# Copies of the transposed activations on VectorE, and later copies, earlier loads and an earlier PSUM layout on the way into a decoder's RWKV-7 scan

## The chip, the core and the metric

One NeuronCore of a Trainium2 chip runs the whole program. The metric is device time in microseconds (us), from start to end of one execution. The core's engines are TensorE (PE in the profile; PEld is its weight load), VectorE (DVE), ScalarE (ACT), GpSimd (POOL) and SyncE (SP), which here issues nearly all DMAs. Each engine runs its own instructions in order; semaphores order the engines against each other.

## The reference

A decoder trunk of two layers in float32, for one sequence of 1024 tokens with 1024 channels. Each layer adds three blocks to the residual x, each between two RMS norms:

```python
x += post_norm(mixer(pre_norm(x)))             # layer 0: RG-LRU, layer 1: RWKV-7
x += post_norm(mem_xattn(pre_norm(x), norm(mem)))
x += post_norm(sqrelu_mlp(pre_norm(x)))        # square(relu(h @ w_up)) @ w_down
```

The RWKV-7 mixer of layer 1 mixes each token with the one before it, and projects the mixes to r, k and v. The decay, the rate a and the gate come from small low-rank maps. Then there is a state of 64×64 for each of 16 heads, and a recurrence over all tokens:

```python
xx = x_prev - x
r = (x + xx * mu[0]) @ w_rkv[0]
k = (x + xx * mu[2]) @ w_rkv[1]
v = (x + xx * mu[3]) @ w_rkv[2]
...
sa = einsum('bhij,bhj->bhi', state, a_t)
state = state * w_t + sa * b_t + v_t * k_t     # outer products
y_t = einsum('bhij,bhj->bhi', state, r_t)
```

## The kernel before, in words

**Arithmetic and buffers.** Each float32 operand of a matrix product is split into a high part (a cast, L233 on ScalarE) and a low part (the difference, L234 on VectorE); a product is three matmuls, high by high (L318), high by low (L319) and low by high (L320). The working buffers are one pool of 45 units u of 128×1024 floats and two large tiles z. PSUM is used in pairs of banks (p, 128×1024) and in single banks (q, 128×512).

**Order of the work.** The program is one straight stream of instructions; a scheduler with a model of the engines reorders each engine's queue, within the data dependences and within constraints such as `behind()`, which lets what is written in it be issued only after what the program has so far. Weights come in the order in which they are used: `self.depth` says for how many weights ahead the split may run and `self.ahead` how many more may be loaded (L249, a DMA on SyncE). `DA = (2, 1)` holds in k and r.

**The seam.** The last product of layer 0's MLP leaves its result transposed tile by tile. For each 128 tokens `tail` computes an RMS norm (L327 squares and sums on ScalarE, L329 and L331 on GpSimd take the root), scales (L673), adds the residual row block that L654 has loaded (L674), stores it (L675), takes a second norm and scales (L681). Every four such blocks go to `transpose_in`: TensorE transposes them (L359) into eight PSUM banks of 128×512, and from each bank ScalarE writes the high part (L362) and, as `raw` is given here, a whole copy into z (L364); the low part comes from GpSimd for odd k (L366, from the copy) and from VectorE for even k (L368, from PSUM). So there are first transposes (tokens 0 to 511) and second ones. They feed the low-rank maps (q, L318 to L320; L1292 copies a result out of PSUM).

**k, r and v.** `rwkv_make_mix` makes the token mixes from the raw tiles z (L1217 on ScalarE, L1220 on VectorE, then the split). `fphase` computes 128 output channels at a time, f = 0 to 7, with 48 matmuls into one pair of banks. k runs in seven turns (`TURNS`, the last with f = 6 and 7), r in six, v in seven. In k, L1349 and L1350 take a result from PSUM; then come decays (stored by L1341), and Gram matrices (L1405, L1406; stored by L1412 and L1413), from which 32×32 triangular systems are solved on GpSimd, and the last set of them on VectorE in small steps (L1433, L1435). In r, L1519 takes a result from PSUM, times the decay that L1515 has loaded, and L1520 stores it.

**The steps beside.** `aside(step)` is called after every turn, and starts those of the steps below whose number stands in the table: `SL`, `SO` and `ST` give the turns in which the four sets are loaded, solved and stored, `ML`, `ME` and `MS` those of the merges (loads L1458 to L1460, matmuls L1472 and L1479). `solve_store` is a copy on ScalarE (L1445, 64×1024) and two stores on SyncE (L1446, L1447).

```python
SL, SO, ST = (2, 5, 8, 9), (2, 5, 8, 9), (5, 8, 12, 13)
```

**The scan** goes in 16 chunks of 64 tokens. For a pair of chunks n, `load` fetches keys (L1624) and the mixed values (L1627, into z), `load_solved` the solved systems (L1638), and `load_late` the values of v and the gates (L1651, L1655), all on SyncE. In v they stand behind the stores L1596 of each phase. GpSimd scales the next chunk's keys (L1668), TensorE forms its Gram matrices (L1679), and the state is read (L1796), solved (L1802) and updated (L1809); L1816 and the copy L1818 give the chunk's output. With PSUM layout "banks" the scan has two sets of four banks, even chunks' outputs in one, odd chunks' in the other; "mixed", which follows for the output projection, keeps the first set and makes two pairs of the rest.

## Time and profile before

| | |
|---|---|
| three runs | 2873.09, 2865.99, 2872.57 us; median 2872.57 |
| the profiled execution | 2871.51 us |
| its span, first to last instruction | 2869.8 us |
| mean granted TensorE clock | 0.993 |
| TensorE busy | 2779.0 us (97%) |
| VectorE, ScalarE, GpSimd busy | 1845.2, 1431.3, 913.3 us |
| idle before the second transposes (TensorE, 1324.84) | 4.58 us |
| idle before r (1488.66), before v (1604.07) | 2.13, 3.63 us |
| idle in the scan (1777.50) | 5.54 us |

How to read it: a row of a timeline gives the start in us from the span's start, the duration, the engine, the line of the kernel, the operation, what it writes and reads, and in brackets how long the engine had been idle and what ended that. "x4" merges neighbours of the same kind. A duration may overlap the next start, since engines are pipelined. SPq is SyncE issuing a DMA; its duration is the issue, not the transfer.

### The profile page before, as it was taken

Reading aid. Unit: us, or ns where it says so; the run is one execution under the profiler, and the core shown is the slowest. Engines: PE = TensorE matmul, PEld = TensorE weight load, DVE = VectorE, ACT = ScalarE, POOL = GpSimd, SP = SyncE. Lnnn points to the kernel's source line nnn. Section 1 sums busy time; section 2 is a strip of 40 time slices with the busy share of each in tenths; the row PEclk is TensorE's granted clock in tenths of the full one; section 3 lists DMA queues with packets and bytes.
Section 4 is the critical chain, followed back from the end, with each engine's and each line's share of the span. In section 5 each row is a group of like instructions: output and inputs, shape, how many; then the busy total and the mean of one; then the engine's idle time right before and its main releaser. Section 6 shows DMA issues by size and latency. Waiting matters only on the chain.

```text
span 2869.8 us, 42738 instructions
## 1 busy us (share of the span) xinstructions
PE 2779.0 (97%) x16955; PEld 2320.8 (81%) x16955; DVE 1845.2 (64%) x2004; ACT 1431.3 (50%) x2203; POOL 913.3 (32%) x962
## 2 busy tenths in 40 slices
PE   7999999999999999998999898999999999999998
PEld 6888788888888888887777687888888888888886
DVE  5577556557455577886575834785665655467778
ACT  5456344546544543438562544663463644555333
POOL 2000114023666500013188223863303276640001
PEclk9999999999999999999999999999999999999999
DMA  8212352323445654433557798963132255464453
GB/s 263 74 45 81 100 168 74 103 81 103 157 152 161 213 188 165 154 111 103 166 158 199 194 254 244 236 164 103 63 106 91 88 171 161 139 240 167 147 176 118
DMA packets 383592, 421.92 MB, mean 147 GB/s; under 512 B 91184, under 2 KB 294176, under 8 KB 383392
## 3 DMA queue, kind: packets, MB, share of 16 engines
q1 hardware_dynamic: 371360, 379.19, 43.7%
q0 software_dynamic: 11568, 39.41, 3.8%
q8 instruction: 133, 2.18, 0.3%
q14 instruction: 67, 0.55, 0.1%
q10 hardware_dynamic: 464, 0.59, 0.1%
HBM read 283.79 MB, written 134.74 MB: 146 GB/s over the span
## 4 chain that ended last, share of the span: by engine, by line
PE 81%; DVE 5%; POOL 3%; ACT 3%; DMA 3%; issue 3%; SPq 2%; ACTq 0%; DVEq 0%; POOLq 0%
PE q L318 17%; PE q L320 17%; PE q L319 17%; PE p L318 8%; PE p L320 8%; PE p L319 8%; PE q L1679 1%; DMA u<-d 1%; DVE u L234 1%; POOL u L1435 1%; ACT u L233 1%; DMA u<-in_b_w_rkv 1%; POOL w L1433 1%; PE q L1796 1%; ACT u L327 1%
## 5 line engine op out<-in xcount | busy, mean ns | idle before, releaser
L234 DVE TENSOR_TENSOR u<-u,u 128x1024 fp32r<-128x1024 f32 (+1 forms) x602 | 809.2, 1375 | 370.9 <-ACT u L233 342.2
L233 ACT CAST u<-u 128x1024 fp32r<-128x1024 f32 (+1 forms) x602 | 591.8, 1020 | 436.6 <-DVE u L1060 224.5
L318 PE MATMUL q<-u,u 128*128 128x512 f32 (+1 forms) x1952 | 744.2, 383 | 5.3 <-ACT u L233 2.4
L319 PE MATMUL q<-u,u 128*128 128x512 f32 (+1 forms) x1952 | 745.8, 382 | 0.5 <-POOL u L366 0.5
L320 PE MATMUL q<-u,u 128*128 128x512 f32 (+1 forms) x1952 | 740.4, 382 | 0.8 <-DVE u L234 0.8
L318 PE MATMUL p<-u,u 128*128 128x512 f32 (+1 forms) x1472 | 554.9, 379 | 18.9 <-DVE u L1519 5.6
L319 PE MATMUL p<-u,u 128*128 128x512 f32 (+1 forms) x1472 | 552.9, 376 | 3.6 <-DVE u L234 3.6
L320 PE MATMUL p<-u,u 128*128 128x512 f32 (+1 forms) x1472 | 552.2, 375 | 3.4 <-DVE u L234 3.4
L329 POOL TENSOR_SCALAR s<-s 128x1 f32<-128x1 f32 x98 | 43.1, 440 | 1268.6 <-ACT u L327 1266.9
L318 PEld LDWEIGHTS q<-u,u 128*128 128x128 f32 x1952 | 367.0, 188 | 77.3 <-ACT u L233 3.5
L320 PEld LDWEIGHTS q<-u,u 128*128 128x128 f32 x1952 | 366.9, 188 | 72.1 <-DVE u L234 1.0
L319 PEld LDWEIGHTS q<-u,u 128*128 128x128 f32 x1952 | 367.0, 188 | 71.6 <-POOL u L366 1.0
L318 PEld LDWEIGHTS p<-u,u 128*128 128x128 f32 x1472 | 280.8, 191 | 72.8 <-ACT u L233 10.6
L320 PEld LDWEIGHTS p<-u,u 128*128 128x128 f32 x1472 | 280.9, 191 | 55.0 <-DVE u L234 5.6
L319 PEld LDWEIGHTS p<-u,u 128*128 128x128 f32 x1472 | 280.9, 191 | 54.5 <-DVE u L234 7.6
L441 POOL TENSOR_TENSOR u<-u,u 128x512 f32<-128x512 f32 x120 | 186.0, 1555 | 8.9 <-PE q L319 5.1
L1118 DVE TENSOR_TENSOR z<-z,q 128x512 f32<-128x512 f32 x192 | 130.6, 683 | 80.9 <-PE q L320 80.9
L318 PE MATMUL q<-z,u 128*128 128x512 f32 x320 | 124.9, 390 | 1.6 <-ACT u L233 1.6
L319 PE MATMUL q<-z,u 128*128 128x512 f32 x320 | 124.5, 389 | 0.0
L320 PE MATMUL q<-z,u 128*128 128x512 f32 x320 | 124.2, 389 | 0.0
L442 POOL TENSOR_TENSOR u<-u 128x512 f32<-128x512 f32 x40 | 76.0, 1899 | 145.3 <-DVE u L234 73.1
L1015 POOL TENSOR_TENSOR u<-u,u 128x512 f32<-128x512 f32 x32 | 46.0, 1438 | 176.3 <-ACT u L1004 166.4
(250 smaller groups left out, 3332.7 us busy)
## 6 DMA issues: line engine op xcount, KB each, us to landing
u<-d SPq DMA_DIRECT2D x194, 512.0 KB, 4.7
d<-u SPq DMA_DIRECT2D x109, 512.0 KB, 3.3
d<-u POOLq DMA_DIRECT2D x68, 512.0 KB, 3.5
d<-u SPq DMA_DIRECT2D x132, 256.0 KB, 3.7
u<-in_m_w_up SPq DMA_DIRECT2D x64, 512.0 KB, 5.4
u<-in_m_w_down SPq DMA_DIRECT2D x64, 512.0 KB, 7.9
u<-in_c_w_kv SPq DMA_DIRECT2D x32, 512.0 KB, 6.4
u<-in_b_w_rkv SPq DMA_DIRECT2D x24, 512.0 KB, 6.7
```

Of the source, the lines that this page charges most:

```text
L233: self.nc.scalar.copy(hv, src)
L234: (eng or self.nc.vector).tensor_tensor(lv, src, hv, ALU.subtract)
L318: mm(o, ah, bh, start=first, stop=False, **kw)
L319: mm(o, ah, bl, start=False, stop=False, **kw)
L320: mm(o, al, bh, start=False, stop=last, **kw)
L327: nc.scalar.activation(junk, src, AF.Square, accum_out=ss)
L329: nc.gpsimd.tensor_scalar(v, ss, 1.0 / n, eps, ALU.mult, ALU.add)
L441: sub = lambda o, x, y: nc.gpsimd.tensor_tensor(o, x, y, ALU.subtract)
L442: nc.gpsimd.tensor_tensor(s[:, a], f1[:, a], f1[:, b], ALU.add)
L1015: tt(s1, r21, r22, ALU.add)
L1118: nc.vector.tensor_add(to_, to_, o)
L1433: eng.tensor_tensor(tv, xv_[:, 0:n, s:s + 1].broadcast_to([128, n, m]), Lv[:, s:s + 1, s + 1:].broadcast_to([128, n, m]), ALU.mult)
```

## The change

Six edits, at five places of the program:

1. In the seam, the whole copies move from ScalarE to VectorE: all eight of the first transposes, every second one (even k) of the second.
2. `solve_store` of the first two sets is called a turn later.
3. In k's turn 5 (f = 5) one more weight may be loaded ahead.
4. In r's turn 4 (f = 5) likewise.
5. The scan's `load(1)` is called after v's turn with f = 6 and `load_solved(1)` behind v's last turn; in chunk 0 only `load_late(1)` is left.
6. The PSUM layout "mixed" is made ahead of chunk 15 and not behind the scan.

```diff
@@ transpose_in
             nc.scalar.activation(h, o, AF.Copy, scale=gc)
             if raw is not None:
-                nc.scalar.activation(raw(k), o, AF.Copy, scale=gc)
+                if k in copies:
+                    nc.vector.tensor_scalar(raw(k), o, gc, None, ALU.mult)
+                else:
+                    nc.scalar.activation(raw(k), o, AF.Copy, scale=gc)
@@ tail, turn
-            xt.append(self.transpose_in(xs, nextg, None if raw is None else (lambda k: raw[hf][:, k, :])))
+            xt.append(self.transpose_in(xs, nextg, None if raw is None else (lambda k: raw[hf][:, k, :]),
+                                        copies=range(0, KT, 1 + hf)))
@@ tables
-SL, SO, ST = (2, 5, 8, 9), (2, 5, 8, 9), (5, 8, 12, 13)
+SL, SO, ST = (2, 5, 8, 9), (2, 5, 8, 9), (6, 9, 12, 13)
@@ k
+        self.depth, self.ahead = DA if i != 5 else (DA[0], DA[1] + 1)
         self.fphase(I["b_w_rkv"][0, 1], fs, xk, prep)
@@ r
+        self.depth, self.ahead = DA if i != 4 else (DA[0], DA[1] + 1)
         self.fphase(I["b_w_rkv"][0, 0], fs, xr, evac_r, spread=i == 0)
@@ v and scan
         if fs[-1] == 6:
             load_solved(0)
+            load(1)
+    with self.behind():
+        load_solved(1)
...
     for c in range(16):
+        if c == 15:
+            self.psum_layout("mixed")
         if c % 2 == 0:
             with (ExitStack() if c else self.behind()):
-                load(c // 2 + 1)
-                load_solved(c // 2 + 1)
+                if c:
+                    load(c // 2 + 1)
+                    load_solved(c // 2 + 1)
                 load_late(c // 2 + 1)
...
     post_norm(15)
     self.depth, self.ahead = 2, 3
-    self.psum_layout("mixed")
```

In the changed program the same code stands a few lines further down: L368 is L371, L673 is L677, L1217 is L1221, L1349 is L1353, L1445 is L1449, L1515 is L1520 and L1520 is L1525. VectorE's copy is L365.

VectorE's queue at the first transposes; q are the transposed PSUM banks, z_7699 the raw tile, and colt holds the gain. Before:

```order
L1118 TENSOR_TENSOR z_7700<-z_7700,q_9462 128x512
L368 SCALAR_TENSOR_TENSOR u_9959<-q_9963,colt,u_9955 128x512
L368 SCALAR_TENSOR_TENSOR u_9960<-q_9979,colt,u_9956 128x512
L368 SCALAR_TENSOR_TENSOR u_9961<-q_9995,colt,u_9957 128x512
L368 SCALAR_TENSOR_TENSOR u_9962<-q_10011,colt,u_9958 128x512
L673 SCALAR_TENSOR_TENSOR u_10027<-z_7700,s_10032,u_5461 128x1024
```

And now, at the same place of VectorE's queue:

```order
L365 TENSOR_SCALAR z_7699<-q_9963,colt 128x512
L371 SCALAR_TENSOR_TENSOR u_9959<-q_9963,colt,u_9955 128x512
L365 TENSOR_SCALAR z_7699<-q_9964,colt 128x512
L365 TENSOR_SCALAR z_7699<-q_9979,colt 128x512
L371 SCALAR_TENSOR_TENSOR u_9960<-q_9979,colt,u_9956 128x512
L365 TENSOR_SCALAR z_7699<-q_9980,colt 128x512
L365 TENSOR_SCALAR z_7699<-q_9995,colt 128x512
L371 SCALAR_TENSOR_TENSOR u_9961<-q_9995,colt,u_9957 128x512
L365 TENSOR_SCALAR z_7699<-q_9996,colt 128x512
L365 TENSOR_SCALAR z_7699<-q_10011,colt 128x512
L371 SCALAR_TENSOR_TENSOR u_9962<-q_10011,colt,u_9958 128x512
L365 TENSOR_SCALAR z_7699<-q_10012,colt 128x512
```

Eight copies have come between and behind the four low parts, and the eight L364 are gone from ScalarE's queue there; L677 (L673 before) follows.

ScalarE's queue towards the end of k, before: L1445 is the first set's copy, the casts after it are weights, p are the results of f = 6 and 7.

```order
L1358 ACTIVATE u_11508<-u_11503 128x1024
L1445 COPY u_10994<-u_10995 64x1024
L233 CAST u_11641<-u_11440 128x1024
L233 CAST u_11647<-u_11639 128x1024
L1217 ACTIVATE u_11701<-z_7699,omu 128x512 x2
L1217 ACTIVATE u_11706<-z_7699,omu 128x512 x2
L233 CAST u_11711<-u_11701 128x1024
L233 CAST u_11715<-u_11706 128x1024
L1349 ACTIVATE u_11775<-p_11651,nkk 128x1024
L1349 ACTIVATE u_11778<-p_11652,nkk 128x1024
```

And now on ScalarE, where the dots leave out the next mixes:

```order
L1362 ACTIVATE u_11510<-u_11505 128x1024
L233 CAST u_11638<-u_11440 128x1024
L233 CAST u_11644<-u_11446 128x1024
L1221 ACTIVATE u_11698<-z_7699,omu 128x512 x2
L1221 ACTIVATE u_11703<-z_7699,omu 128x512 x2
L233 CAST u_11708<-u_11698 128x1024
L233 CAST u_11712<-u_11703 128x1024
L1353 ACTIVATE u_11772<-p_11648,nkk 128x1024
L1353 ACTIVATE u_11775<-p_11649,nkk 128x1024
...
L1362 ACTIVATE u_11892<-u_11772 128x1024
L1449 COPY u_10994<-u_10995 64x1024
L233 CAST u_11911<-u_11642 128x1024
```

The copy has moved behind the casts, the mixes and the two results, some 25 instructions further back.

SyncE's queue in r around the weights (in_b_w_rkv); the DMAs with d as source are loads of what the kernel has stored, L1458 to L1460 the merge's. Before:

```order
L249 DMA u_12515<-in_b_w_rkv 128x8x128
L1520 DMA d_10150<-u_12513 128x1024
L1459 DMA u_12660<-d_10155 32x16x32
L1460 DMA u_12660<-d_10152 32x512
L1458 DMA u_12658<-d_10154 32x16x32 x4
L1459 DMA u_12660<-d_10155 32x16x32
L1460 DMA u_12660<-d_10152 32x512
L1486 DMA d_10146<-u_12346 128x1024
L1515 DMA u_12670<-d_10149 128x1024
L1515 DMA u_12672<-d_10149 128x1024
L249 DMA u_12674<-in_b_w_rkv 128x8x128
L249 DMA u_12680<-in_b_w_rkv 128x8x128
```

And now on SyncE:

```order
L249 DMA u_12515<-in_b_w_rkv 128x8x128
L249 DMA u_12521<-in_b_w_rkv 128x8x128
L1525 DMA d_10150<-u_12513 128x1024
L1463 DMA u_12662<-d_10155 32x16x32
L1464 DMA u_12662<-d_10152 32x512
```

The first of the two L249 behind the merge loads now stands ahead of them, right behind the L249 before.

More of the change, by code (lines that the diff above doesn't have):

```diff
@@ L347, in half, with transpose_in @@
         return [(at(h, k), at(l, k)) for k in range(KT)]
-    def transpose_in(self, xs, g, raw=None, dst=None):
+    def transpose_in(self, xs, g, raw=None, dst=None, copies=()):
         nc = self.nc
```

## The prediction

> **What bounds the kernel now.** I read the page first, then TensorE's timeline over the stretches that the change touches, then the other engines' timelines back from each wait of TensorE.
>
> ```profile
> span 2869.8 us, 42738 instructions
> PE 2779.0 (97%) x16955; PEld 2320.8 (81%) x16955; DVE 1845.2 (64%) x2004; ACT 1431.3 (50%) x2203; POOL 913.3 (32%) x962
> ```
>
> TensorE is busy 2779.0 of 2869.8 us, and the change takes no matmul away. So all it can win is idle time of TensorE, 90.8 us in the whole span, and whatever a wait costs behind itself. TensorE's timeline where the change acts:
>
> ```profile
> 1324.84 4.62 PE L359 MATMUL q<-ident,u 128*128 128x128 f32 x24 [4.58 <-ACT u L1292]
> 1330.19 1.09 PE L359 MATMUL q<-ident,u 128*128 128x128 f32 x8 [0.74 <-DVE u L368]
> 1332.50 0.50 PE L318 MATMUL q<-u,u 128*128 128x512 f32 x1 [1.22 <-DVE u L368]
> ...
> 1488.66 0.51 PE L318 MATMUL p<-u,u 128*128 128x512 f32 x1 [2.13 <-DVE u L1350]
> 1488.97 0.63 PE L319 MATMUL p<-u,u 128*128 128x512 f32 x1
> 1489.39 0.63 PE L320 MATMUL p<-u,u 128*128 128x512 f32 x1
> ...
> 1492.61 0.39 PE L319 MATMUL p<-u,u 128*128 128x512 f32 x1
> 1492.84 0.39 PE L320 MATMUL p<-u,u 128*128 128x512 f32 x1
> ...
> 1519.10 0.47 PE L318 MATMUL p<-u,u 128*128 128x512 f32 x1 [1.18 <-DVE u L1519]
> ...
> 1599.23 1.20 PE L1472 MATMUL q<-u 32*32 32x32 f32 x64
> 1604.07 0.47 PE L318 MATMUL p<-u,u 128*128 128x512 f32 x1 [3.63 <-DVE u L1519]
> ...
> 1777.50 2.08 PE L1679 MATMUL q<-z,u 64*128 64x128 f32 x16 [5.54 <-DMA u<-d]
> ...
> 1920.64 0.50 PE L318 MATMUL p<-u,u 128*128 128x512 f32 x1 [0.92 <-ACT u L1818]
> ```
>
> The number in brackets is TensorE's idle time and what ended it: 4.58 us in the seam, 2.13 between k and r, 3.63 between r and v, 5.54 in the scan, 0.92 at its end. There is a second price. Behind the 2.13 us gap matmuls start 0.42 us apart (1488.97, 1489.39), later 0.23 apart (1492.61, 1492.84): some eight or nine run at half rate, 9 × 0.2 = 1.8 us more. The matmuls behind the 1.18 us at 1519.10 start at that pace too, so removing most of a gap without getting below about 1 us does not win this back.
>
> [...]
>
> **Part 1, copies to VectorE.** The seam's first transposes end a chain that leads to the second ones:
>
> ```profile
> 1295.25 0.69 ACT L362 ACTIVATE u<-q,colt 128x512 fp32r<-128x512 f32 x1 [1.58 <-PE q L359]
> ...
> 1304.39 1.18 ACT L327 ACTIVATE u<-z 128x1024 f32<-128x1024 f32 x1
> 1304.69 1.30 POOL L366 TENSOR_TENSOR u<-z,u 128x512 fp32r<-128x512 f32 x1 [1.03 <-ACT z L364]
> 1306.94 1.29 DVE L673 SCALAR_TENSOR_TENSOR u<-z,s,u 128x1024 f32<-128x1024 f32 x1 [2.69 <-POOL s L331]
> 1310.14 2.35 DVE L674 TENSOR_TENSOR u<-u,u 128x1024 f32<-128x1024 f32 x2
> 1318.00 1.23 DVE L674 TENSOR_TENSOR u<-u,u 128x1024 f32<-128x1024 f32 x1 [0.21 <-DMA u<-d]
> 1323.87 0.75 DVE L681 TENSOR_SCALAR u<-u,s 128x1024 f32<-128x1024 f32 x1 [0.72 <-POOL s L331]
> L390 DVE TENSOR_SCALAR u<-q,colt x16: 741/746/751, 383.9 to 2253.3; 128x512 f32<-128x512 f32 x16
> L368 DVE SCALAR_TENSOR_TENSOR u<-q,colt,u 128x512 fp32r<-128x512 f32 x8 | 6.0, 751 | 10.3 <-ACT z L364 10.3
> ```
>
> ScalarE runs 16 instructions from 1295.25, 0.57 us apart (16 × 0.57 = 9.1, to 1304.39), and only then the squares L327 that the next RMS norms wait for. Eight fewer bring L327 forward by 8 × 0.57 = 4.6 us. VectorE takes eight copies, of the form of L390 (0.746 us), between its four L368 (0.751 us). At full length 12 × 0.75 = 9.0 us, to 1304.3; with the 0.1 us by which neighbours overlap (two L674 take 2.35, one 1.23) 12 × 0.65 = 7.8, to 1303.1. Both are before 1306.94, where L673 starts now. I take 1303.1: the first L673 moves by 3.8 us; the second, at its end, by 4.6 us, and so does the first pair of L674 at 1310.14. Its stores, the loads of the residual rows behind them on SyncE, the L674 at 1318.00 that waits for such a load, and the last L681 follow. GpSimd has four L366 of 1.30 us either way; in the new order the small rsqrt steps stand between them, so they don't wait for the last.
>
> In the second transposes ScalarE has three instructions a pair instead of four; over three pairs 3 × 0.57 = 1.7 us of the 0.74 + 1.22 = 1.96 us of waits for L368. Sum for the seam 4.6 + 1.7 = **6.3 us**. Bounds: 3 (12 full-length DVE operations give 1304.3, 2.6 us, and a little of the rest) and 8 (4.58 + 0.74 + 1.22 is 6.5, and 1.5 of half rate behind them).
>
> Do the copies slow GpSimd, or it them? The nearest rows:
>
> ```profile
> 1500.82 1.64 DVE L234 TENSOR_TENSOR u<-u,u 128x1024 fp32r<-128x1024 f32 x1
> ...
> 1597.78 1.22 DVE L234 TENSOR_TENSOR u<-u,u 128x1024 fp32r<-128x1024 f32 x1 [6.68 <-ACT u L233]
> ```
>
> L234 takes 1.64 us while the solves run on GpSimd and 1.22 alone. The same third on 12 operations would be 12 × 0.65 × 0.34 = 2.7 us; that too is inside the bound of 3. I take nothing, since the copy reads one operand from PSUM, like L368, which kept 0.75 beside L366. [...]
>
> **Part 2, the solves' copies a turn later; part 3, a weight more ahead in k.** ScalarE and VectorE between k and r:
>
> ```profile
> 1476.62 2.06 ACT L1445 COPY u<-u 64x1024 f32<-64x1024 f32 x1 [11.26 <-POOL u L1435]
> ...
> 1484.45 2.08 PE L1405 MATMUL q<-u,u 64*64 64x64 f32 x64
> 1485.71 2.11 ACT L1349 ACTIVATE u<-p,nkk 128x1024 f32<-128x1024 f32 x2
> 1487.36 2.29 DVE L1350 TENSOR_TENSOR u<-u,p 128x1024 f32<-128x1024 f32 x2
> 1489.56 3.29 DVE L1220 SCALAR_TENSOR_TENSOR u<-z,colt,u 128x511 f32<-128x511 f32 x4
> ...
> 1517.75 2.34 DVE L1519 TENSOR_TENSOR u<-u,p 128x1024 f32<-128x1024 f32 x2
> ```
>
> ScalarE stands 11.26 us at L1445 for GpSimd's solve, with the casts, the mixes L1217 and the evacuations L1349 queued behind it; TensorE waits for L1350 behind those. In the new order L1445 is behind all of them. The second L1349 then starts when its matmuls are done, at 1484.45 (TensorE's L1405, 2.08 us, begins there and ends at 1486.53). Now it starts at 1485.71 + 2.11 / 2 = 1486.76, and the first L1350 at 1487.36; one turn of L1349 alone, the first long done, leaves L1350 off TensorE's path. VectorE's mixes L1220 start when the second L1349 is over, 1484.45 + 1.05 = 1485.5, and the first of their inputs is there, about 1486, not 1489.56: **3.6 us**, by VectorE's own chain, which I take to be full up to the L1519 of 1517.75. The gap of 2.13 us and its 1.8 us of half rate give 3.9, so VectorE's chain, not TensorE, sets this. Bounds 2 (the gap goes, the half rate stays) and 5.5 (1.18 at 1519.10 shrinks below 1 us, with half its 1.8). The stall at 1519.10 stays: L1519 remains in VectorE's order behind the same work. L1445's own 2.06 us and its two stores go to a time where the solve's readers are turns away: nothing; 2 us if ScalarE is then needed. The extra weight in k, loaded ahead of SyncE's L1341 and L1394, sets the next cast's input early; no cast waited for one there (the idle 11.26 us is L1445's), so alone it is worth nothing, and its risk is the slower rival.
>
> **Part 4, a weight more ahead in r.**
>
> ```profile
> 1573.39 0.43 SPq L249 DMA_DIRECT2D u<-in_b_w_rkv  x1
> ...
> 1588.80 1.41 SPq L249 DMA_DIRECT2D u<-in_b_w_rkv  x2
> 1596.70 1.05 ACT L233 CAST u<-u 128x1024 fp32r<-128x1024 f32 x1 [12.27 <-DMA u<-in_b_w_rkv]
> ...
> 1602.70 1.22 DVE L1519 TENSOR_TENSOR u<-u,p 128x1024 f32<-128x1024 f32 x1
> 1607.84 1.21 DVE L1519 TENSOR_TENSOR u<-u,p 128x1024 f32<-128x1024 f32 x1
> ```
>
> The cast of v's weight holds ScalarE 12.27 us, then VectorE 6.68 us (the row of 1597.78), and the L1519 that frees PSUM for v is behind them. One of the two L249 of 1588.80 now stands right behind that of 1573.39, 15 us sooner, though it may wait for its buffer. At the 7.9 us from issue to cast (1588.80 to 1596.70) the cast could come at 1582; ScalarE and VectorE then do the mixes, while TensorE is still in r. L1519 of a phase can run when its matmuls are done, the last at 1599.23: I put the first at 1598.5 to 1599.5 instead of 1602.70 and the second, behind it and a few mixes, at about 1604. TensorE could go on at 1600.43, when L1472 ends (1599.23 + 1.20): 3.63 us plus 1.8 us of half rate is 5.4; VectorE's mixes are late next, so I take **4 us**, bounds 0 and 7.
>
> **Part 5, scan loads.**
>
> ```profile
> 1761.07 5.77 SPq L1627 DMA_DIRECT2D z<-d  x4
> ...
> 1770.65 6.49 SPq L1624 DMA_DIRECT2D u<-d  x4
> 1777.62 1.04 POOL L1668 TENSOR_TENSOR u<-u,pc 128x512 f32<-128x512 f32 x1 [7.38 <-DMA u<-d]
> ```
>
> Chunk 2's rows L1624 take 6.49 us to issue, and start 9.6 us after L1627; TensorE and GpSimd wait for them. Issued during v's sixth phase they have landed, and only L1655 and L1651 are left there. On SyncE they go past the stores L1596 of two phases, whose readers come only in the scan: nothing, or 2 us if a buffer isn't free yet. The whole 5.54 us goes. A 5.54 us gap costs at least the half rate that stands behind 2.13 us, 1.8. Sum **7.3 us**, bounds 5 (the 7.3 less such 2 us) and 8.
>
> **Part 6, the PSUM layout moved** ahead of the last chunk takes the 0.92 us at 1920.64 away; the last chunk has fewer banks, and may wait 1 us for one, under a VectorE that is late anyway: **0.9 us**, bounds −1 and 1.
>
> Sum: 6.3 + 3.6 + 4 + 7.3 + 0.9 = 22.1 us. The profiled execution took 2871.5 us and the three runs 2866.0 to 2873.1, median 2872.6; 2871.5 − 22 is 2849.5, and from the median 2850.4: I say **2850**. Bounds of the terms together: all low 9 us (2863), all high 29.5 us (2842).
>
> **The rivals.** *Half comes off:* the next late thing stands right behind. VectorE's mixes, in an order that still has L1519 behind them, take back what k, r and v gained; the scan and the seam's lower bound remain: 7.3 + 3 + 0.9 = 11 us, **2860**. For it: the stall at 1519.10, where L1519 is late behind VectorE's own work. Against: at 1604.07 L1519 was late behind a load (12.27 us at the cast), and that goes.
>
> *No change:* TensorE's early starts are given back where data comes at fixed times, as at the scan's DMA: **2870**. Against: the scan's own wait goes too.
>
> *Slower:* the extra L249 finds no free buffer and holds SyncE's queue until a phase of matmuls has freed one. In r everything between the L249 of 1573.39 and those of 1588.80 stands behind it: L1520, the merge loads and L1515. L1472 at 1599.23 needs the merge loads; issued by 1588.80 and with 7.9 us to land they have 1599.23 − 1588.80 − 7.9 = 2.5 us to spare, and from there each microsecond of the hold is one of TensorE. Held until r's last matmuls are done, 15 us later than the turn before, it costs some 15 us; in k the same extra weight stands ahead of the Gram stores which the solves read, and a hold of one phase, 48 matmuls × 0.23, costs 11. Seam, scan and end still give 6.3 + 7.3 + 0.9 = 14.5: 2871.5 + 26 − 14.5, **2883**. For it: 45 buffers are shared by everything. Against: SyncE issued both L249 of 1588.80 in 1.41 us, without a wait.
>
> **How the numbers follow.** Under 0.3% (8.6 us) this kernel's runs can't tell a change. Forecast 0.63, half 0.20, no change 0.11, slower 0.06. Faster by over 0.3% (under 2864) is 0.63 + 0.20 = 0.83; same 0.11, slower 0.06. The range runs from 2840 (all terms high, and 2 us for runs that differ by 7) to 2863 (all terms low, which holds the half rival), and leaves out the last two, 0.17.
>
> **What would show it.** Right: TensorE's 4.58, 2.13, 3.63 and 5.54 us gaps are below 1 us or gone, the seam's first L327 starts right behind eight L362, L1445 stands behind L1349, no 12 us wait at a cast before v, and 1.18 at 1519 stays. Wrong: a new wait of TensorE over 3 us, a SyncE hole behind the extra L249, or copies over 0.9 us.

## The result, and the profile after

The changed kernel takes 2861.62 us (median of 12 runs, 2858.27 to 2868.18); the kernel before took 2872.17 beside it (12 runs, 2865.99 to 2876.83). The ratio is 0.9966, 95% interval [0.9958, 0.9975]: 0.34% faster, 10.5 us where 22 were forecast. The profiled execution took 2861.18 us, its span is 2859.5 us against 2869.8.

To see where the 10.5 us come from, I follow single matmuls: the same one in both traces bounds a stage, and what the stage has become shorter is the gain there. These are the busy times by stage, of the kernel before, in its stages: the seam, k, r, r's last merge matmuls, r's end to the first part of v, v's end, the scan. The columns are the stage, its length, the busy time of TensorE, its weight load, VectorE, ScalarE and GpSimd with their instructions, the granted TensorE clock, DMA share and rate.

```profile
1282.79:1333.76 50.97, 42.85 (x210) 35.05 (x208) 32.16 (x38) 33.71 (x59) 23.84 (x31) 0.97 0.57 185
1333.76:1478.80 145.04, 144.17 (x964) 113.81 (x963) 95.87 (x99) 94.70 (x128) 55.57 (x72) 1.00 0.50 141
1478.80:1571.55 92.75, 87.43 (x604) 71.34 (x602) 63.08 (x67) 37.51 (x49) 75.80 (x104) 0.96 0.62 175
1571.55:1593.70 22.15, 20.44 (x265) 16.55 (x264) 18.63 (x30) 4.51 (x7) 14.96 (x25) 1.00 0.73 192
1593.70:1657.73 64.03, 54.66 (x414) 42.16 (x412) 49.81 (x76) 41.17 (x57) 7.94 (x12) 0.97 0.77 207
1657.73:1741.60 83.87, 81.89 (x915) 68.23 (x914) 27.60 (x30) 35.36 (x51) 21.19 (x33) 0.98 0.92 247
1741.60:1920.64 179.04, 166.46 (x3276) 146.68 (x3274) 122.00 (x227) 101.16 (x395) 113.38 (x132) 0.98 0.95 227
```

And of the changed kernel, between the same matmuls:

```profile
1282.54:1329.94 47.40, 43.43 (x209) 34.66 (x208) 40.75 (x51) 27.68 (x49) 24.10 (x31) 0.96 0.61 199
1329.94:1481.04 151.10, 147.70 (x964) 116.08 (x963) 103.49 (x108) 98.56 (x132) 57.81 (x74) 0.98 0.50 139
1481.04:1570.61 89.57, 85.87 (x604) 70.12 (x602) 54.58 (x56) 33.51 (x42) 78.08 (x107) 0.98 0.60 168
1570.61:1596.11 25.50, 22.77 (x266) 18.66 (x264) 24.57 (x41) 12.20 (x18) 10.56 (x19) 0.87 0.81 223
1596.11:1649.94 53.83, 52.04 (x413) 41.41 (x412) 43.09 (x68) 33.80 (x48) 7.92 (x12) 1.00 0.87 248
1649.94:1735.76 85.82, 83.37 (x915) 69.53 (x914) 27.59 (x30) 35.30 (x51) 21.12 (x33) 0.96 0.89 243
1735.76:1909.13 173.37, 166.58 (x3276) 147.00 (x3274) 120.56 (x227) 100.07 (x393) 111.88 (x131) 0.98 0.96 226
```

The lengths differ by −3.6, **+6.1**, −3.2, **+3.3**, **−10.2**, +2.0 and −5.7 us; what follows, up to the matmul at 2239.77 us (2229.05 now), adds 0.8, and the sum is −10.5. Length less PE busy is idle time. Where PE busy grows with the same number of matmuls I count the growth as half rate: the clock column falls with it (k 1.00 to 0.98, the merge 1.00 to 0.87), and in k the granted clock is 0.50 from 1429.10 to 1435.93. So k lost 2.5 us to waiting (0.87 to 3.40 idle) and 3.5 to half rate (144.17 to 147.70). So two losses, of 6.1 us in k and 3.3 at r's merge, stand there that no term of the sum held.

TensorE's waits in the changed kernel, in the timeline:

```profile
1322.63 1.14 PE L359 MATMUL q<-ident,u 128*128 128x128 f32 x8 [0.65 <-ACT u L1296]
...
1429.16 1.64 PE L1332 MATMUL q<-u,u 64*128 64x512 f32 x5 [3.40 <-DVE u L1410]
...
1502.92 0.50 PE L319 MATMUL p<-u,u 128*128 128x512 f32 x1 [1.86 <-DVE u L234]
...
1519.76 0.47 PE L318 MATMUL p<-u,u 128*128 128x512 f32 x1 [1.25 <-DVE u L1524]
...
1576.90 1.89 PE L1476 MATMUL q<-u 32*32 32x32 f32 x62 [2.73 <-DMA u<-d]
...
1601.64 1.20 PE L1476 MATMUL q<-u 32*32 32x32 f32 x64
1602.77 0.50 PE L318 MATMUL p<-u,u 128*128 128x512 f32 x1
...
1711.42 0.22 PE L1483 MATMUL q<-u,u 32*32 32x32 f32 x2 [2.11 <-issue]
...
1774.25 0.45 PE L1796 MATMUL q<-u,u 128*64 128x64 f32 x2 [2.25 <-DMA u<-d]
```

The four waits that were to go (4.58, 2.13, 3.63, 5.54 us) are 0.65 us or gone; v's first matmul at 1602.77 waits for nothing. In their place stand 3.40 us in k at the matmuls behind the Gram matrices, 2.73 at r's merge for a load, 2.11 at v's end that the profile puts down to "issue" (nothing that it shows), and 2.25 in the scan for a load.

At the wait in k, TensorE needs a bank that VectorE frees: L1406 (L1410 in the changed kernel) takes the Gram matrices out of PSUM, times small decays db that a load brings. First the kernel before, then the changed one:

```profile
1432.83 1.29 DVE L1406 TENSOR_TENSOR u<-q,db 128x512 f32<-128x512 f32 x2 [6.81 <-DMA db<-d]
1433.58 0.97 PE L1328 MATMUL q<-u,u 64*128 64x512 f32 x5 [0.87 <-DVE u L1406]
...
1428.41 1.29 DVE L1410 TENSOR_TENSOR u<-q,db 128x512 f32<-128x512 f32 x2 [6.84 <-DMA db<-d]
```

In both kernels VectorE starts 12.0 us behind the start of the Gram matrices (1420.87 and 1416.43). So the load has not become later; what differs is how much work TensorE has meanwhile.

### The profile page after: what moved, and what is told of

It is laid out like the page before. It is cut to its first block, busy times and chain, and to the rows that moved or that the text cites. A ratio compares the mean times of both kernels' runs of the same rounds, so it can differ in the third digit from the quotient of the medians.

```text
span 2859.5 us, 42726 instructions
## 1 busy us (share of the span) xinstructions
PE 2782.0 (97%) x16955; PEld 2322.7 (81%) x16955; DVE 1850.8 (65%) x2016; ACT 1424.5 (50%) x2191; POOL 912.0 (32%) x962
## 4 chain that ended last, share of the span: by engine, by line
PE 87%; DVE 4%; ACT 3%; issue 2%; POOL 2%; DMA 1%; SPq 1%; DVEq 0%; POOLq 0%; ACTq 0%
PE q L318 17%; PE q L319 17%; PE q L320 17%; PE p L318 9%; PE p L320 9%; PE p L319 9%; PE q L1685 1%; DVE u L234 1%; ACT u L233 1%; PE q L1796 1%; PE q L1808 1%; PE q L1332 1%; POOL s L331 1%; ACT u L952 1%; PE q L1709 1%
## 5 line engine op out<-in xcount | busy, mean ns | idle before, releaser
L234 DVE TENSOR_TENSOR u<-u,u 128x1024 fp32r<-128x1024 f32 (+1 forms) x602 | 808.7, 1374 | 348.4 <-ACT u L233 323.8
L329 POOL TENSOR_SCALAR s<-s 128x1 f32<-128x1 f32 x98 | 41.2, 421 | 1268.9 <-ACT u L327 1266.3
```

What stands on the lines that cost most here:

```text
L234: (eng or self.nc.vector).tensor_tensor(lv, src, hv, ALU.subtract)
L329: nc.gpsimd.tensor_scalar(v, ss, 1.0 / n, eps, ALU.mult, ALU.add)
```

## The experiments

The theory at the outset: the parts of the change do what they say, and two side effects take back about half: with the copies, the scheduler's model puts TensorE's queue in another order in k, 25 matmuls of f = 4 ahead of those (L1328, now L1332) that need the banks which VectorE's L1406 (L1410) frees, where before and without the copies there are 36; and DMAs stand in another order on SyncE. The rival: the gains aren't there to be had, since later data comes at fixed times and takes back whatever is won ahead of it.

One table for all of them: the change of each stage against before, in us, between the same matmuls, each from one profiled execution. "k to v" sums four stages. Ratios are to be compared, not times: the kernel before, measured beside each set of runs, had medians from 2872.17 to 2875.51 us.

| run | seam | k | r | merge | v | k to v | v end | scan | ratio to before, 95% |
|---|---|---|---|---|---|---|---|---|---|
| the change | −3.6 | +6.1 | −3.2 | +3.3 | −10.2 | −4.0 | +2.0 | −5.7 | 0.9966 [0.9958, 0.9975] |
| copies alone | −3.4 | +5.8 | +3.5 | −1.0 | −0.7 | +7.6 | −0.7 | +0.6 | 1.0023 [1.0014, 1.0033] |
| all but the copies | +1.6 | +0.7 | −4.9 | +5.0 | −5.6 | −4.8 | +1.7 | −6.1 | 0.9975 [0.9964, 0.9985] |
| scan loads alone | +0.5 | −0.2 | 0.0 | −0.2 | −0.8 | −1.2 | +1.0 | −5.8 | 0.9997 [0.9986, 1.0007] |
| r's weight alone | +0.4 | −0.1 | −2.0 | +2.2 | −1.5 | −1.4 | +3.5 | +1.1 | 0.9975 [0.9965, 0.9984] |
| second store back | −1.1 | +5.7 | −2.5 | +4.0 | −10.3 | −3.1 | +2.0 | −7.2 | 0.9967 [0.9955, 0.9978] |
| even copies | −2.9 | +0.2 | −3.4 | +3.9 | −5.0 | −4.3 | +1.1 | −4.9 | 0.9957 [0.9945, 0.9970] |
| late values | −3.3 | +6.0 | −3.2 | +3.6 | −9.4 | −3.0 | −1.5 | −9.6 | 0.9959 [0.9946, 0.9972] |
| early decays | −3.6 | +4.6 | −2.9 | +4.2 | −9.9 | −4.0 | +6.3 | −3.4 | 0.9969 [0.9958, 0.9980] |
| even + late | −2.0 | +0.4 | −3.0 | +3.0 | −4.7 | −4.3 | +0.8 | −6.5 | 0.9951 [0.9938, 0.9963] |
| even + late + small weights | −2.3 | −1.5 | −5.7 | +5.3 | −2.6 | −4.5 | −1.9 | −9.5 | 0.9951 [0.9936, 0.9967] |
| even + late + decays | −2.7 | +1.2 | −1.6 | −1.8 | −5.5 | −7.7 | +1.7 | −6.3 | 0.9952 [0.9936, 0.9968] |
| all three | −2.4 | −1.1 | −2.8 | +4.4 | −8.2 | −7.7 | −0.2 | −3.1 | 0.9942 [0.9930, 0.9954] |

The scan's column, from −3.1 to −9.6 among versions that differ little there, and v's end show how far one execution is from another; the medians behind the ratios stand on five and more.

**Copies alone** (part 1 on the kernel before).

```
+                if k in copies:
+                    nc.vector.tensor_scalar(raw(k), o, gc, None, ALU.mult)
+                else:
+                    nc.scalar.activation(raw(k), o, AF.Copy, scale=gc)
...
+                                        copies=range(0, KT, 1 + hf)))
```

> Part 1 alone: the copies on VectorE, all else as before. Two theories on why the seam's gain (the same matmul 3.8 us earlier after the seam) was gone by the end of k. Order theory: the scheduler, whose model sees the copies elsewhere, puts 25 matmuls of k ahead of the banks that VectorE's L1410 frees, not 36, so TensorE waits there about 3.4 us and has a half-rate stretch behind it: the same matmul is 3.8 to 4.5 us earlier at 1425 us and 1 to 2.5 us later at 1460; total within 3 us of before (2869 to 2875). Fixed-time theory: what k waits for (the small db loads) comes at a fixed time whoever is early, so a shift is given back but not overdrawn: 0 at 1460, total 2872.

Measured: 2877.37 us against 2872.49, slower, and above the totals of both theories. The seam's 3.4 us are there and k loses 5.8. On TensorE in k, then at r's start:

```profile
1430.04 1.64 PE L1332 MATMUL q<-u,u 64*128 64x512 f32 x5 [3.10 <-DVE u L1410]
...
1495.91 0.77 PE L318 MATMUL p<-u,u 128*128 128x512 f32 x1 [6.26 <-DVE u L1354]
```

The wait in k comes with the copies alone, though the last copy runs 100 us ahead of it. The second row is new: 6.26 us before r, where 2.13 stood. L1354 stands behind a cast of ScalarE, which waits for a weight; SyncE issues that one behind the two stores of the solve (L1450, L1451, issued by 1477.04):

```profile
1477.13 3.91 SPq L249 DMA_DIRECT2D u<-in_b_w_rkv  x2
```

```profile
1484.95 1.05 ACT L233 CAST u<-u 128x1024 fp32r<-128x1024 f32 x1 [9.09 <-DMA u<-in_b_w_rkv]
```

Part 2, which moves those stores back, and part 3, which moves such a load forward, are missing here; the two were not tried apart.

**All but the copies** (parts 2 to 6).

```
-            if k in copies: ... nc.vector.tensor_scalar(raw(k), o, gc, None, ALU.mult)
+            nc.scalar.activation(raw(k), o, AF.Copy, scale=gc)
```

> All parts but the copies. Order theory: the 36 matmuls of k are there, so no new wait at L1406 in k (0.9 us as before); the same matmul is 0 at 1460, 2 to 4 us earlier in r's first phase, 3 us later again at the merge L1472 in r where 6 more matmuls stand ahead of it, 5 to 8 us earlier in v, and 9 to 12 us earlier behind the scan: total 2860 to 2863, as good as the whole change. Fixed-time theory: the early part gains are the same with and without the copies; total the same as the whole change too, but with a wait of 2 us or more at L1406 again.

Measured: 2864.24 against 2872.49, a little above the 2860 to 2863 of the order theory. k keeps its time (+0.7), r and v gain, and the wait at the merge's loads is there without the copies, 4.14 us. So k's loss and the merge's have two causes.

**Scan loads alone** (part 5 on the kernel before).

```
         if fs[-1] == 6:
             load_solved(0)
+            load(1)
+    with self.behind():
+        load_solved(1)
...
-                load(c // 2 + 1)
-                load_solved(c // 2 + 1)
+                if c:
+                    load(c // 2 + 1)
+                    load_solved(c // 2 + 1)
```

> Part 5 alone: the scan's loads for chunks 2 and 3 earlier. By the prediction 7.3 us (2865). By the trace of the changed kernel 5.7 us (2866 to 2867): the 5.54 us wait for L1624 goes and one of about 2.3 us for the values of v (L1651) comes, one chunk later, with a slow stretch behind it, because SyncE issues the loads of L1627 for chunks 4 to 7 (7.4 us) ahead of L1655 and L1651. If instead it gives nothing, the scan is bound by DMA bytes.

Measured: 2870.72 against 2872.49, ratio 0.9997, no difference. In the profiled execution the scan gains 5.8 us, and 2.2 of it are lost behind. A wait of 1.79 us for a load (at L1788 of this run's kernel, which is L1796 of the changed one) has come at 1779.61: the keys are there, the values of v aren't. So the two forecasts of the total both failed; that the scan is bound by DMA bytes is not shown either, since the wait for the keys went.

**R's weight alone** (part 4 on the kernel before).

```
+        self.depth, self.ahead = DA if i != 4 else (DA[0], DA[1] + 1)
         self.fphase(I["b_w_rkv"][0, 0], fs, xr, evac_r, spread=i == 0)
```

> Part 4 alone: a weight more ahead in r. The prediction took 4 us; in the whole change and in the run without copies the same matmul gained 5.5 to 10 us between r's end and v's second phase. If that is this part's own, total 2864 to 2867, with the 3.6 us wait before v gone and the 2.8 us one at L1570 smaller. If it was only a recovery of what r had lost just before, 0 to 3 us: total 2870 to 2872.

Measured: 2866.79 against 2875.51, ratio 0.9975, as the first theory has it: this one part gives as much as parts 2 to 6 together (0.9975 too). Its profiled execution, at 2875.89 us, was the slowest of its 12, so its row of the table tells of the start of v only (the matmul at 1604.07 comes 3.7 us sooner against that at 1593.70) and not of the total. The 2.84 us wait of the kernel before at L1570, in v, did not shrink: it is 4.09 here.

**Second store back** (the whole change, one number of a table).

```
-SL, SO, ST = (2, 5, 8, 9), (2, 5, 8, 9), (6, 9, 12, 13)
+SL, SO, ST = (2, 5, 8, 9), (2, 5, 8, 9), (6, 8, 12, 13)
```

> The whole change, but the second set's solve_store in its old turn (ST = 6, 8, 12, 13). Order theory: the merge L1472 in r stands behind 66 + 12 matmuls again and not 76 + 8; SyncE's merge loads are not held by a later L1520; TensorE's wait at that merge falls from 2.7 to about 1 us with its half-rate stretch, so the same matmul is 3 us earlier than in the whole change from 1585 us on if v does not give it back: total 2858 to 2859. Rival: the loads land at the DMA's rate, the wait stays 2.7 us and the total 2861 to 2862.

Measured: 2862.53 against 2872.49. TensorE's order in r is that of before, and the wait is still there. The order of TensorE isn't its cause; that theory falls. It is on SyncE and VectorE, in the changed kernel:

```profile
1557.18 0.35 SPq L1450 DMA_DIRECT2D d<-u  x1
...
1564.16 0.36 SPq L1520 DMA_DIRECT2D u<-d  x1
...
1569.46 0.33 SPq L1525 DMA_DIRECT2D d<-u  x1
...
1573.31 0.49 SPq L1463 DMA_DIRECT2D u<-d  x1
```

VectorE there, with the idle time ahead of L1524 (put down to an older matmul; for the same instruction, the run with even copies has 6.25 us for a load):

```profile
1568.21 1.22 DVE L1524 TENSOR_TENSOR u<-u,p 128x1024 f32<-128x1024 f32 x1 [5.93 <-PE q L1476]
```

The decay's load L1520 is issued at 1564.16, L1524 multiplies by it at 1568.21, L1525 stores the product at 1569.46, and the merge's loads stand behind that store on SyncE until 1573.8; TensorE comes to them at 1574.17 and waits to 1576.90. Without the stores L1450 and L1451 ahead of it TensorE waits 3.47 us in this run, since the chain itself is what is late.

**Early decays** (the whole change, r's decays loaded one turn sooner).

```
-    for i, fs in enumerate([[0, 1], [2], [3], [4], [5], [6, 7]]):
-        for f in fs:
-            early(f)
+    rturns = [[0, 1], [2], [3], [4], [5], [6, 7]]
+    for f in rturns[0]:
+        early(f)
+    for i, fs in enumerate(rturns):
+        for f in rturns[i + 1] if i < 5 else []:
+            early(f)
```

> The whole change, with r's decay loads L1515 called a turn earlier. If SyncE's queue sets the pace in r (decay load, L1519, store L1520, merge loads behind it, L1472), L1519 no longer waits for its load, the merge loads are issued 1 to 3 us earlier and TensorE's wait of 2.7 us at the merge (1577 us) falls below 1 us: total 2857 to 2859. If that wait is one of DMA landing times alone, it stays at 2 to 4 us: total 2861 to 2863.

Measured: 2865.52 against 2875.51. VectorE's product and TensorE's merge matmuls in this run:

```profile
1556.20 1.22 DVE L1524 TENSOR_TENSOR u<-u,p 128x1024 f32<-128x1024 f32 x1 [3.34 <-PE p L320]
```

```profile
1574.07 1.17 PE L1476 MATMUL q<-u 32*32 32x32 f32 x62 [0.47 <-DMA u<-d]
1583.29 0.24 PE L1483 MATMUL q<-u,u 32*32 32x32 f32 x2 [2.16 <-ACT u L1478]
```

L1524 comes 12 us sooner, when its matmuls are done, and the merge's wait is 0.47 us: the chain decay, product, store, merge loads is shown as the cause. But the copy L1478 out of PSUM is late next, 9 us on, "k to v" is −4.0 as in the change, and the ratio is no better.

**Even copies** (the whole change, copies of even k only, in both halves; TensorE's order in k has 36 matmuls again).

```
-                                        copies=range(0, KT, 1 + hf)))
+                                        copies=range(0, KT, 2)))
```

> The whole change, but the copies of even k alone go to VectorE in both transposes (four and four instead of eight and four). In this order the scheduler puts 36 matmuls of k ahead of the banks, as before the change, not 25. Order theory: the wait of 3.4 us for L1410 in k falls below 1 us and the shift that the seam gave is kept to the end of k (the same matmul 2 to 4 us earlier at 1478 us instead of 2.2 later); r takes part of that back at the merge; total 2856 to 2859. Rival, that VectorE's copies cost the time themselves or that k's loads land at a fixed time: the wait is there again, total 2861 to 2864.

Measured: 2864.02 against 2875.51. TensorE in k, at r's merge and in v:

```profile
1431.16 0.96 PE L1332 MATMUL q<-u,u 64*128 64x512 f32 x5 [1.04 <-DVE u L1410]
...
1573.02 1.88 PE L1476 MATMUL q<-u 32*32 32x32 f32 x62 [3.67 <-DMA u<-d]
...
1633.10 2.05 PE L1576 MATMUL q<-center,u 128*128 128x128 f32 x8 [3.65 <-DVE u L1595]
```

k's loss is gone, +0.2 instead of +6.1 us, with one number in the code of the seam: the order of TensorE's queue is its cause. Yet the profiled executions of both versions end within 0.9 us of each other (span 2860.4 and 2859.5). What k keeps, v no longer gains: −5.0 instead of −10.2. Ahead of the last row's L1595 VectorE waits for loads (L1607 and L1609, all issued by 1619.48):

```profile
1631.07 1.28 DVE L1566 SCALAR_TENSOR_TENSOR u<-u,colt,u 128x1024 f32<-128x1024 f32 x1 [2.59 <-DMA u<-d]
```

The changed kernel, which comes to v 4.3 us later (1596.11, here 1591.80), starts the same L1566 at 1631.85 without a wait: the early start is given back at a load. The time is that of the rival, and by the ratio's interval it is not told apart from the change.

**Late values** (the whole change; the loads L1633 of the mixed values of two later pairs held back behind what is needed first).

```
-        for w in range(2):
-            nc.sync.dma_start(mv[:, :, w, :], MVd[:, :, w, ts])
+        with (self.behind() if n in (2, 3) else ExitStack()):
+            for w in range(2):
+                nc.sync.dma_start(mv[:, :, w, :], MVd[:, :, w, ts])
```

> The whole change, with the loads L1627 for chunks 4 to 7 held behind the loads for chunks 2 and 3 on SyncE. If the 2.25 us wait for the values at 1774 us comes from these 7.4 us of issue ahead of L1655 and L1651, it goes, with its slow stretch of 2 us: the scan gives 8 to 10 us instead of 5.7, total 2857 to 2859. If the values land at the DMA's rate or wait for their stores, the wait stays and the total is 2861 to 2863.

Measured: 2863.60 against 2875.51. The wait at 1774 is gone and the scan gains 9.6 us in the profiled execution, which at 2855.95 was the fastest of six. By the ratio's interval it is not told apart from the change.

**Combinations.** All of them have the even copies and the late values. The first has nothing else.

> The whole change with two edits that were tried apart: copies of even k only in both halves, and the scan's mixed values of chunk pairs 2 and 3 loaded later. TensorE's order in k has 36 matmuls ahead of the Gram matrices, as before. Theory 'each wait has its own cause': no gap over 1.5 us at 1429, TensorE stands about 2.4 us ahead of before at k's end (2.2 behind in the whole change), the 2.25 us wait in the scan at 1774 is gone; the scan itself gives 9 us (5.7 in the whole change); 2.5 + 3.5 us better than the whole change, ratio to before about 0.9945. Rival 'given back': what k keeps is lost at the merge's loads in r and at the matmul of L1576 in v, 3.7 us each as with even copies alone; only the scan's 3.5 us remain, ratio 0.996.

Measured: 2860.97 against 2874.21. The rival is right on k to v: 3.31 us at the merge, 3.92 at L1576, −4.3 in all. The scan keeps 6.5 us and not 9.

The second loads the small weights b_w2 and b_a2 before the seam:

```
+    self.wa2raw = raw = self.unit()
+    self.nc.sync.dma_start(raw[0:64, :], I["b_w2"][0])
+    self.nc.sync.dma_start(raw[64:128, :], I["b_a2"][0])
```

> As the run with even copies and late values, and the small weights b_w2 and b_a2 that ScalarE casts just ahead of the second transposes are loaded before the seam and not in it. Theory 'the seam's second transposes wait for that load next': ScalarE's cast at 1321 waits for no DMA (0.69 us in the whole change, 2.67 in another run of these copies), TensorE's shift after the seam is 1 to 3 us better than in the run with which it shares the rest, and varies less. Rival 'the chain of norms sets it': the last L685 at 1321.3 and the transposes behind it stay where they are, the shift after the seam is the same within 0.5 us. By either the rest of the program keeps its waits; ratio 0.9935 by the first, as the other run by the second.

Measured: 2859.22 against 2874.21. ScalarE and TensorE in the seam:

```profile
1314.12 1.04 ACT L233 CAST u<-u 128x1024 fp32r<-128x1024 f32 x1
```

```profile
1322.53 0.55 PE L359 MATMUL q<-ident,u 128*128 128x128 f32 x3 [1.29 <-DVE u L685]
...
1324.81 1.11 PE L359 MATMUL q<-ident,u 128*128 128x128 f32 x4 [1.01 <-DVE u L685]
```

The cast comes 7 us sooner than in the changed kernel and waits for nothing, and the seam gains 2.3 us where its neighbour gains 2.0: the transposes wait for L685, the end of the chain of norms, instead. Rival right.

The third loads the decays a turn sooner, with the diff above.

> As the run with even copies and late values, and r's decays are loaded a turn sooner, so that fewer DMAs stand in SyncE's queue ahead of the merge's loads. Theory 'SyncE's queue sets the merge's wait': the wait of 3.5 us for a DMA at 1573 to 1580 is gone, and with k's order kept, TensorE is 6 us or more ahead at v's start (1604). Rival 'VectorE and GpSimd set v': what is won is given back inside r and v, in a gap of 2 us or more at a copy out of PSUM (L1483 on ScalarE) and at L1597, and the scan starts no sooner than in the run that shares the rest; the ratio is then the same within 0.001.

Measured: 2860.23 against 2874.21. The merge's wait, 3.31 us without, is gone (a merge 9 us ahead of it waits 1.16, 1.03 without), and now k to v is −7.7, 3.4 more than without. The profiled execution keeps that to its end (2857.57 us against 2861.00), though it has a wait of 3.40 us put down to "issue" at 1710; in the medians it does not show, the ratio is that of the run without.

The fourth has all three.

> Even copies, late values, the small weights before the seam and the decays a turn sooner, all together. Theory 'each wait has its own cause': the shifts add up, seam 5 us, k nothing lost, r's merge nothing lost, v 5 to 9, scan 9: about 20 us before the output projection, ratio 0.993. Rival 'given back': VectorE's and GpSimd's chains set v's end; the shift at 1741 is 6 to 8 us as in the other runs, plus the scan's 9: 16 us, ratio 0.9945 to 0.996.

Measured: **2858.49 us** against 2874.21 (5 runs, 2856.60 to 2859.90), ratio 0.9942 [0.9930, 0.9954], the best of all versions, 15.7 us below before. Its interval does not meet that of the change. Neither theory had its size: k to v gains 7.7 as in the third, the shift at 1741 is 9 us, and the scan gives 3.1 only, with five waits of 0.8 to 1.6 us put down to "issue" between 1791 and 1827.

## Why the prediction was wrong

**The order of the queues, costed at nothing.** The step that failed first is that part 1 was costed only where its copies run. Its place in the model of the scheduler also decides how many matmuls cover the wait for the Gram matrices in k, 130 us later: 11 fewer, at 0.23 us each 2.5 us, are the 2.5 us of idle time there, and half rate behind them takes 3.5. Shown by the copies alone and the even copies. The prediction looked at the new order at three places, and not at this one; its own sign of being wrong, a new wait of TensorE over 3 us, stands here. Yet this step alone is not what the sum lost: with k's order kept, k to v is −4.3 instead of −4.0.

**"VectorE's mixes are late next, so I take 4".** Parts 2, 3 and 4 were given 3.6 and 4 us. Singly they look right or too small (r −3.2, v −10.2), but a merge wait and k's loss stand against them, and what stays from k to v is 4.0. In eight versions with part 4's weight and parts 2 and 3, with k's loss or without it, this sum lies between −3.0 and −4.8: what is kept in one stage is missing in the next. Only where k's order was kept *and* the decays came sooner did it become −7.7, in both such runs, where 7.6 were forecast. So the step that failed is to add the two terms up as if each wait stood alone: either of two costs that the sum put at nothing, the order in k and the decay's chain in r, keeps the stretch near −4. The rivals by which early starts are given back, to VectorE's mixes or "where data comes at fixed times", were right about this stretch: SyncE's and VectorE's chains set its end, and the decays' is one of them. That the first rival's 2860 is so near 2861.62 is luck: it has nothing from k to v, where 4.0 were measured, and 7.3 from the scan, where 5.7 were. In v it is given back at L1595, behind an L1566 that waits 2.59 us for a load with even copies and 2.83 with late values too; what sets that load's time was not taken apart. In the ratios the 3.4 us more do not show: 0.9951 without the decays, 0.9952 and 0.9942 with them.

**"Its two stores go to a time where the solve's readers are turns away: nothing".** The readers were the wrong thing to look at. The stores stand on SyncE ahead of a decay's load, which is issued at 1564.16 (1562.56 before), with a chain of four steps behind it that ends at TensorE. That chain had to be followed; it is late without the stores too, as the run with the second store back shows.

**The seam, 6.3 forecast, 3.6 measured.** ScalarE's step was right: L327 starts at 1299.56, 4.8 us sooner (4.6). So was the second one, 1.6 us in the second transposes (1.7). Between them the chain lost two, here on VectorE and GpSimd in the changed kernel:

```profile
1303.62 1.27 DVE L677 SCALAR_TENSOR_TENSOR u<-z,s,u 128x1024 f32<-128x1024 f32 x1
1305.33 2.31 DVE L677 SCALAR_TENSOR_TENSOR u<-z,s,u 128x1024 f32<-128x1024 f32 x1 [0.44 <-POOL s L331]
1307.57 2.35 DVE L678 TENSOR_TENSOR u<-u,u 128x1024 f32<-128x1024 f32 x2
```

```profile
1303.63 1.67 POOL L331 TENSOR_TENSOR s<-s,nhalf 128x1 f32<-128x1 f32 x1
1305.27 1.28 POOL L369 TENSOR_TENSOR u<-z,u 128x512 fp32r<-128x512 f32 x1
```

The twelve operations end at 1303.62, where 1303.1 was forecast. But the first L677 now runs beside L331, which takes 1.67 us instead of 0.55, and the second beside the last L369 (L366 before), and takes 2.31 instead of 1.27. "GpSimd has four L366 of 1.30 us either way ... so they don't wait for the last" was the failed step: they don't wait for it, but L331 and L677 take longer in the new order, each beside an instruction of the other engine. The kernel before has such a case, L329: 1.29 us at 1306.99, beside the L673 of 1306.94, and 0.19 at 1306.08. L678 moved by 2.6 us, not 4.6, and with it the tail. The copies themselves were as I said, 0.74 us beside L369. The two differ in their inputs, a z and a u for the L677 of 2.31 us, a PSUM bank for the copy of 0.74; whether that is the reason was not tried.

**The scan, 7.3 forecast, 5.7 measured.** The 5.54 us go, as forecast. The loads of v's values, L1657, stand behind four L1633 of the mixed values (L1627 before), which take 7.40 us to issue, and TensorE waits 2.25 us for them: "only L1655 and L1651 are left there" left out L1633. Scan loads alone and late values show both halves. The half rate that the term counted as won did not go: it lasts 6.83 us behind the 2.25 us wait (granted clock 0.50 from 1773.85 to 1780.68), as it did behind the 5.54 (0.50 from 1775.67 to 1782.50). And of the 5.7 us, 0.9 are part 6's wait, which ends this stage, and 1.3 a wait put down to "issue" (at 1809.16 before) that this execution does not have.

**Part 6, 0.9 forecast, nothing measured.** The wait of 0.92 us before the output projection is gone (1909.12 starts at once), and TensorE waits 0.51 us for L234 two matmuls later; in every version with part 6 what follows the scan is 0.8 to 1.0 us longer, with copies alone and r's weight alone 0.0 and 0.1. Part 6 was not tried alone, and scan loads alone, without it, lose 2.2 there.

**Half rate.** The forecast took 1.8 us of half rate as the price of the 2.13 us ahead of it. That was right only in part: half rate followed 2.13 us of idle time (granted clock 0.50 from 1488.95 to 1492.36 before), but in the traces it lies on a fixed grid and does not start with the gap; see the last section. The stall at 1519 stayed, as forecast (1.25 us), but its half rate went (granted clock 1.00 from 1517.85 to 1524.68).

Of what the prediction called right: the extra weights held up nothing (SyncE issued the two L249 at 1575.80 in 1.06 us), L1449 stands behind L1353, and no cast waits 12 us before v. The sum missed by 11.6 us: 2.7 in the seam, 3.6 from k to v, 2.0 at v's end, 1.6 in the scan and 1.7 at its end.

## What to carry to other kernels

Where a scheduler with a cost model orders the queues, an edit's price stands anywhere in the program: compare each engine's whole order before and after, and ask of each wait how many instructions now cover it. A wait that goes is worth only as much as the next chain behind it allows; follow that chain to its DMA before adding up the waits, and sum over the whole stretch up to the next wait for a load. Look for a store in front of loads on the same queue: here SyncE stood from 1565.0 to 1569.5 us ahead of the store L1525, whose data L1524 made from 1568.21 to 1569.43, and the merge's loads came behind it.

## What the runs showed of the hardware

In the two traces the half-rate stretches lie on a fixed grid. Matmuls of the changed kernel at the ends of three of them, where the duration falls from 0.63 (or 0.58) to 0.47 us or less:

```profile
1302.22 0.63 PE L318 MATMUL q<-u,u 128*128 128x512 f32 x1
1302.65 0.47 PE L320 MATMUL q<-u,u 128*128 128x512 f32 x1
...
1582.29 0.58 PE L318 MATMUL p<-u,u 128*128 128x512 f32 x1
1582.72 0.39 PE L319 MATMUL p<-u,u 128*128 128x512 f32 x1
...
1718.83 0.58 PE L319 MATMUL p<-u,u 128*128 128x512 f32 x1
1719.25 0.39 PE L320 MATMUL p<-u,u 128*128 128x512 f32 x1
```

1302.65, 1582.72 and 1719.25 are 280.07 and 136.53 us apart, 82.05 and 40.00 times 3.413 us. That step is read from the granted clock: in the changed kernel the shortest stretches at 0.50 last 3.41 us (1299.40 to 1302.81, 1504.20 to 1507.61), the others between 330 and 2840 us twice that (1429.10, 1575.88, 1712.41 and 1773.85, each for 6.83), and these six starts lie 38.0, 22.0, 21.0, 40.0 and 18.0 steps apart. The ends in the trace of before lie 9.0 and 25.0 such steps apart (1492.36, 1523.08, 1608.42), on a grid shifted against this one. How long the waiting is does not decide it alone: 1.04 and 0.81 us of waiting in the step before 1299.40 stood ahead of half rate, and 1.86 before 1504.20. Two steps of the kernel before, each with the one behind it; the second number is TensorE's busy time, and behind the five engines stands the granted clock:

```profile
1516.26:1519.67 3.41, 2.23 (x39) 2.02 (x39) 3.41 (x3) 0.00 (x0) 3.17 (x4) 1.00 0.92 289
1519.67:1523.09 3.42, 3.42 (x10) 2.64 (x9) 3.42 (x4) 0.00 (x0) 3.18 (x4) 0.50 0.92 220
1639.14:1642.55 3.41, 1.48 (x11) 1.43 (x12) 3.41 (x5) 2.13 (x4) 2.99 (x5) 1.00 0.85 203
1642.55:1645.97 3.42, 3.41 (x20) 2.65 (x18) 3.42 (x4) 1.70 (x3) 0.66 (x1) 1.00 0.88 244
```

With 1.18 us of idle time in one step half rate came in the next, with 1.93 us in another it did not, and neither did it behind the 1.25 us at 1519.76 in the changed kernel. From 330 to 2840 us of the two traces seven steps at full clock have more than 2 us of idle time (2.07 to 3.41 us: before those from 533.22, 1321.70, 1485.54, 1601.59 and 1772.26, now those from 1425.69 and 1709.00), and each has a granted clock of 0.50 in the step behind it. What else counts below that, such as the kind of matmuls in the rest of the step, was not tried. Where half rate comes there it lasts one step or two (two in k, from 1429.10 to 1435.93). As an estimate from the rows of the prediction, 0.42 us from matmul to matmul against 0.23, a step of 3.41 us holds 8 matmuls that take 0.20 us more each, 1.6 us. The granted clock also differs among executions of one kernel: with even copies the shortest has 0.992 (2858.01 us), the longest 0.989 (2873.97 us).

Waits put down to "issue" differ widely too: those over 0.5 us sum to 2.98 us in the profiled execution of the kernel before and to 2.67 in that of the changed one, while with all three the five between 1791 and 1827 alone sum to 6.79.
